# A third buffer for raw modulation weights, and low-part weight pieces loaded one piece earlier and stored one step later, in a two-layer attention and convolution backbone

## The chip, the cores and the metric

One core of a Trainium2 chip runs the whole program. The core has a matrix engine (PE, TensorE), a vector engine (DVE, VectorE), an activation engine (ACT, ScalarE), a general engine (POOL, GpSimd) and a queue engine (SP, SyncE) that here issues nearly all transfers (DMA) between device memory and the on-chip memory. Each engine works through its own instruction list in order and waits on semaphores for the others. The metric is the device time of one execution in microseconds (us); the kernel before takes 1704.04 us, the median of 3 runs (1703.88 to 1704.39).

## The reference, cut to what matters

Two layers: windowed attention with a context prefix, then a convolution module. All of it is fp32. Cut to the parts that the change touches or runs beside:

```python
D_MODEL, SEQ, CTX_LEN = 1024, 1024, 256
N_Q_HEADS, N_KV_HEADS, HEAD_DIM, WINDOW = 16, 4, 128, 128
# layer i: modulation of the tokens from the condition c
shift, scale, gate = split(silu(c) @ ada_w[i] + ada_b[i], 3)
h = rmsnorm(x, norm_g[i]) * (1 + scale) + shift
# layer 0: attention; q, k, v, z are columns of one projection
q, k, v, z = split(h @ attn_w_in)             # k, v also of the context
p = softmax over [sink, 256 context keys, latent keys within +-128]
x = x + gate * ((p @ [v_ctx, v]) * silu(z)) @ attn_w_out   # attn_w_out: 2048 x 1024
# layer 1: gated pointwise, depthwise convolution of width 31, layer norm, swish
x = x + gate * (u * silu(z)) @ conv_w_out                  # conv_w_out: 2048 x 1024
out = rmsnorm(x, final_g)
```

## The kernel before

**Arithmetic.** A matmul operand in fp32 is written as the sum of a high part (the rounding to `F32R`, made by an ACT copy) and a low part (the remainder, a subtraction on POOL or DVE). Each product is then three matmuls: high by high, high by low, low by high. So every weight piece needs an ACT copy and a subtraction before PE can use it.

**The attention stage** is a loop over 128 steps, 16 heads by 8 blocks of 128 queries (L1154). A step issues `scores` of the next block (6 matmuls into a PSUM tile `pss`, a masked maximum on DVE, an exponential on ACT, a scaling of `p_page` on POOL), then 12 matmuls of the next projections (`fill`), every fourth step the product with the values (`pv`), and then `transposes` of this step's block (4 or 5 PE transposes of `p_page` into `pss`, an ACT copy into `pthi`, a DVE subtraction into `ptlo`). PE keeps the program's order there; the other engines are ordered by the scheduler of the framework when the program is built, from its own estimate of times, and that order is then fixed. Where a key and value group ends (after heads 3, 7 and 11) the step is a regrouping: it projects `k` and `v` of the next group (`job`), with an ACT copy `vf_half` of each part of `v` that PE then transposes.

**Two background tasks** are generators that the loop advances by one `yield` a step:

- `ada_rest` (L604) adds up the rest of the modulation, silu(c) @ ada_w, in 128 pieces of 128x256 numbers (128 KB). Each piece is loaded by SP into one of two raw buffers, `dww_raw` and `wsum_raw` (places that the convolution uses later), and then multiplied and added on DVE. The load of piece i+1 is issued in the step that uses piece i; its buffer is the one that piece i-1 was read from.
- `low_parts` (L663) makes the low parts of the two output projections, `attn_w_out` and `conv_w_out`, in 32 pieces of 128x2x512 (512 KB): load into a page `low`, twice an ACT copy into a half page `lhi` and a POOL subtraction back into the page, then a store to device memory (`wolA`, `wolC`), from where later stages read it. A piece takes three turns: in the first the load is issued, and after it the store of the piece before (`store`, L657); in the second and third the two halves are split. A step with no turn for `low_parts` calls `store` (L1170).

**Memory.** `Pages` hands out 45 pages of 4 KB a partition and 6 half pages in rotation: a page is taken from the front of the free list and goes to its end when it is freed. Who gets a page waits for the last reader of its former content. `lhi`, `rope`, `oz` and `vf` share the half pages; `low`, `p`, `wraw` (raw projection weights) and others share the pages.

**SP's queue** holds, in one list, the loads of raw projection weights (`wraw_page`), the modulation pieces, the low pieces, their stores, and the stores `ozd` of the attention's output. An entry that waits holds up all entries behind it.

Of the kernel before, what the change touches and what calls it, by code (L numbers as in the profile page):

```python
# [9 lines left out]
F32 = mybir.dt.float32  # L10
# [4 lines left out]
P = 128  # L15
# [79 lines left out]
def backbone_kernel(  # L95
# [14 lines left out]
    cpool = ctx_stack.enter_context(tc.tile_pool(name="cpool", bufs=1))  # L110
    pgpool = ctx_stack.enter_context(tc.tile_pool(name="pages", bufs=1))
    hfpool = ctx_stack.enter_context(tc.tile_pool(name="halves", bufs=1))
    ps = ctx_stack.enter_context(tc.tile_pool(name="ps", bufs=2, space=PSUM))
    dr = ctx_stack.enter_context(tc.tile_pool(name="dr", bufs=1, space=bass.MemoryType.DRAM))
    pg = Pages(pgpool, 45, "page", 1024)
# [456 lines left out]
    def vt_split(vf, n, dh, dl):  # L572

        tp = ps_o(*vbank)
        for i in range(n // P):
# [16 lines left out]
    acc_a = mask_pg[:, 768:1024]  # L592
    ada_raw = [cpool.tile([P, n], F32, tag=t, name=t + "_raw", bufs=1)[:, 0:256]
               for t, n in (("dww", NJ * TAPS), ("wsum", NJ * 16))]

    anchor = []
    anchor_p = []
# [6 lines left out]
    def ada_rest():  # L604
        todo = [(l, c0) for l, c0 in [(0, 2048 + 256 * i) for i in range(4)] + [(1, 256 * i) for i in range(12)]]
        todo = [(l, c0, kt) for l, c0 in todo for kt in range(KT)]

        def load(i):
            l, c0, kt = todo[i]
            SY.dma_start(out=ada_raw[i % 2], in_=ada_w[l, kt * P:(kt + 1) * P, c0:c0 + 256])  # L610

        load(0)
        bank = ps_o(1)
        acc, o = bank[:, 0:256], bank[:, 256:512]
        for i, (l, c0, kt) in enumerate(todo):
            if i + 1 < len(todo):
                load(i + 1)
            raw = ada_raw[i % 2]
            if kt == 0:
                after(V.tensor_scalar(out=acc, in0=raw, scalar1=cs[:, kt:kt + 1], scalar2=None, op0=ALU.mult))  # L620
                for b in range(2):
                    col = (c0 - 2048 if l == 0 else 1024 + c0) // P + b
                    bs = slice(b * P, b * P + P)
                    stt(acc[:, bs], ident, abt[:, col:col + 1], acc[:, bs], ALU.mult, ALU.add)
            else:
                after(stt(acc, raw, cs[:, kt:kt + 1], acc, ALU.mult, ALU.add))
            yield
            if kt < KT - 1:
                continue
            V.tensor_copy(acc_a, acc)  # L630
            yield "copied"
            if i + 1 == len(todo):
                yield
            if c0 >= 2048:
                PE.matmul(o[0:1], ones[:, 0:1], acc_a, start=True, stop=True)
                V.tensor_copy(acc_a[0:1], o[0:1])
                SY.dma_start(out=gd[l][:, c0 - 2048:c0 - 1792], in_=acc_a[0:1])
            else:
                for b in range(2):
                    PE.matmul(o[:, b:b + 1], acc_a[:, b * P:b * P + P], ones[:, 0:1], start=True, stop=True)  # L640
                V.tensor_copy(mod1[:, c0 // P:c0 // P + 2], o[:, 0:2])

    adag = ada_rest()


# [17 lines left out]
    def low_parts():  # L663

        items = [(pair_rows(w, m, kk), d[m, kk]) for w, d in ((Wo, wolA), (Wp, wolC)) for m in range(2) for kk in range(NK)]
        for src, dst in items:
            raw = pg.alloc(F32, [2, 512], "low")
            SY.dma_start(out=raw, in_=src)
            store()
            yield "open"  # L670
            for b in range(2):
                hi = hp.alloc(F32R, None, "lhi")
                act(hi[:, 0:512], raw[:, b], AF.Copy)
                after(split_lo(G, raw[:, b], raw[:, b], hi[:, 0:512]), anchor_p)
                hp.free(hi)
                if b == 0:
                    yield "open"
            made.append((dst, raw))
            yield "shut"
        store()  # L680

    subs = [(h, m) for h in range(2) for m in range(2)]
    seqB = [(s, kk) for s in range(len(subs)) for kk in range(NK)]
# [1109 lines left out]
```

## Time and profile before

The median of the runs shown is 1704.04 us. The profiled execution took 1702.68 us in itself, of which the span from its first to its last instruction is 1700.9 us. One execution was profiled; all sums are made against it.

| what | number |
|---|---|
| runs, median (lowest to highest) | 1704.04 us (1703.88 to 1704.39) |
| profiled execution, its own time | 1702.68 us |
| its span | 1700.9 us |
| granted clock of PE, mean | 0.999 |
| attention stage | about 75 to 826 us of the span |
| first and last conversion of a low piece | 113.7 and 714.7 us |
| DMA, mean over the span | 143 GB/s |
| low pieces, median from issue to landing | 4.0 us (`attn_w_out`), 4.8 us (`conv_w_out`) |

How to read it: busy time is counted when an instruction of the engine runs. Rows for the DMA queues (SPq, ACTq) stand for the issue of a transfer, not for its duration. In a row of the timeline, the text in brackets is the idle time of that engine just before the instruction and what ended it. Matmuls overlap: a row of 0.39 us is followed by the next matmul 0.23 us later, so a wait of PE shorter than the overlap does not show as idle time.

### The profile page before, as it was taken

The page shows a single profiled execution, that of the slowest core. Times are in us where ns is not written, and L with a number is a line of the kernel's source. Part 1 is how long each engine was busy: PE and PEld are TensorE (multiplying, and loading weights), DVE is VectorE, ACT ScalarE, POOL GpSimd, SP SyncE. Part 2 cuts the span into 40 slices and gives each one's busy share as a digit, 9 for nine tenths or more (in the row PEclk, how much of TensorE's full clock was granted, in tenths as well). Part 3 has the DMA queues.
Part 4 walks back from the last instruction along what each step waited for, and adds up shares of the span by engine and source line. Part 5 has one row for each costly group of instructions (what it writes and reads, how often), then busy time and mean ns, then how long its engine had stood idle before and what let it go on. Part 6 is the DMA issues. An engine that isn't in the chain of part 4 may idle for free.

```text
span 1700.9 us, 23976 instructions
## 1 busy us (share of the span) xinstructions
PE 1684.5 (99%) x8490; PEld 1420.9 (84%) x8490; DVE 1091.3 (64%) x2074; ACT 877.9 (52%) x1538; POOL 882.5 (52%) x732
## 2 busy tenths in 40 slices
PE   9999999999999999999999999999999999999997
PEld 6888888888888888888888888888888888888886
DVE  5755544555355544556215289999999999868922
ACT  6755544555345544446234355665665664566831
POOL 0256653666456554643001167999898888130400
PEclk9999999999999999999999999999999999999999
DMA  9334442444334532437776622010111202377981
GB/s 383 93 100 140 140 124 92 143 155 140 97 119 147 160 121 91 140 118 266 279 252 216 243 81 99 14 62 25 62 63 43 88 32 81 124 266 250 331 271 50
DMA packets 109848, 242.46 MB, mean 143 GB/s; under 512 B 11306, under 2 KB 28002, under 8 KB 109728
## 3 DMA queue, kind: packets, MB, share of 16 engines
q1 hardware_dynamic: 103328, 230.43, 39.7%
q10 hardware_dynamic: 6400, 10.49, 2.5%
q8 instruction: 67, 1.10, 0.3%
q14 instruction: 53, 0.43, 0.1%
HBM read 188.70 MB, written 41.69 MB: 135 GB/s over the span
## 4 chain that ended last, share of the span: by engine, by line
PE 92%; DMA 4%; ACT 1%; issue 1%; DVE 1%; POOL 1%; SPq 0%; ACTq 0%; POOLq 0%; DVEq 0%
PE psg L89 48%; PE pss L89 24%; PE pso L89 20%; DMA araw_page<-in_k_ada_dram 2%; DMA low_page<-in_conv_w_out_dram 1%; DMA rope_half<-rope_half 1%; DMA dww_raw<-in_ada_w_dram 0%; ACT lhi_half L89 0%; POOL rope_half L89 0%; SPq L89 0%; DMA low_page<-in_attn_w_out_dram 0%; DVE ptlo L89 0%; ACT pthi L89 0%; ACT p_page L89 0%; ACT rope_half L89 0%
## 5 line engine op out<-in xcount | busy, mean ns | idle before, releaser
L89 POOL TENSOR_TENSOR odd_half<-odd_half,prod_half 128x513 f32<-128x513 f32 (+2 forms) x252 | 314.2, 1254 | 23.0 <-ACT prod_half L89 9.6
L89 PE MATMUL psg<-hh_page,whi_page 128*128 128x512 f32 x600 | 235.6, 393 | 0.0
L89 PE MATMUL psg<-hl_page,whi_page 128*128 128x512 f32 x600 | 234.5, 391 | 0.0
L89 PE MATMUL psg<-hh_page,wlo_page 128*128 128x512 f32 x600 | 234.0, 390 | 0.0
L89 ACT ACTIVATE prod_half<-ubuf,dww 128x513 f32<-128x513 f32 (+2 forms) x252 | 165.5, 675 | 116.0 <-POOL odd_half L89 112.2
L89 POOL TENSOR_TENSOR wlo_page<-wraw_page,whi_page 128x512 fp32r<-128x512 f32 (+1 forms) x104 | 172.9, 1679 | 92.0 <-ACT whi_page L89 79.6
L89 POOL TENSOR_SCALAR p_page<-p_page,sc 128x640 f32<-128x640 f32 (+1 forms) x128 | 99.3, 776 | 221.2 <-DVE sc L89 215.2
L89 PE MATMUL psg<-h2h_page,whi_page 128*128 128x512 f32 x464 | 181.9, 392 | 0.0
L89 PE MATMUL psg<-h2h_page,wlo_page 128*128 128x512 f32 x464 | 180.6, 389 | 0.0
L89 PE MATMUL psg<-h2l_page,whi_page 128*128 128x512 f32 x464 | 180.6, 389 | 0.0
L89 DVE SCALAR_TENSOR_TENSOR pss<-ubuf,dww,pss 128x512 f32<-128x512 f32 (+3 forms) x270 | 172.8, 673 | 0.1
L89 DVE SCALAR_TENSOR_TENSOR pss<-ubuf,wsum,pss 128x512 f32<-128x512 f32 (+3 forms) x270 | 172.2, 673 | 0.2
L89 DVE TENSOR_TENSOR ptlo<-pss,pthi 128x640 fp32r<-128x640 f32 (+1 forms) x144 | 103.5, 719 | 85.9 <-ACT pthi L89 84.6
L89 ACT ACTIVATE pthi<-pss 128x640 fp32r<-128x640 f32 (+1 forms) x144 | 88.8, 617 | 105.3 <-PE pss L89 98.8
L89 ACT ACTIVATE p_page<-p_page,sc 128x641 f32<-128x641 f32 (+1 forms) x128 | 102.6, 802 | 75.4 <-DVE sc L89 71.7
L89 PEld LDWEIGHTS psg<-hh_page,wlo_page 128*128 128x128 f32 x600 | 112.7, 188 | 24.5
L89 PEld LDWEIGHTS psg<-hh_page,whi_page 128*128 128x128 f32 x600 | 112.7, 188 | 19.4
L89 PEld LDWEIGHTS psg<-hl_page,whi_page 128*128 128x128 f32 x600 | 112.8, 188 | 18.5
L89 ACT ACTIVATE whi_page<-wraw_page 128x1024 fp32r<-128x1024 f32 x88 | 92.6, 1052 | 53.6 <-PE psg L89 19.9
L89 PE MATMUL pso<-h2h_page,whi_page 128*128 128x512 f32 x304 | 118.3, 389 | 0.0
L89 PE MATMUL pso<-h2l_page,whi_page 128*128 128x512 f32 x304 | 118.3, 389 | 0.0
L89 PE MATMUL pso<-h2h_page,wlo_page 128*128 128x512 f32 x304 | 118.3, 389 | 0.0
(254 smaller groups left out, 3999.6 us busy)
## 6 DMA issues: line engine op xcount, KB each, us to landing
wraw_page<-in_k_wconv_dram SPq DMA_DIRECT2D x48, 512.0 KB, 3.3
wraw_page<-in_k_win_dram SPq DMA_DIRECT2D x40, 512.0 KB, 3.8
wol_page<-wolA SPq DMA_DIRECT2D x32, 512.0 KB, 6.3
wo_page<-in_attn_w_out_dram SPq DMA_DIRECT2D x32, 512.0 KB, 5.8
wo_page<-in_conv_w_out_dram SPq DMA_DIRECT2D x32, 512.0 KB, 4.8
wol_page<-wolC SPq DMA_DIRECT2D x32, 512.0 KB, 6.2
rope_half<-rope_half ACTq DMA_DIRECT2D x80, 128.0 KB, 2.4
araw_page<-in_k_ada_dram SPq DMA_DIRECT2D x16, 512.0 KB, 10.3
```

What stands on the lines that cost most here:

```text
L89: r = f(*a, **k)
```

## The change

The raw modulation buffers become three: a tile of 128x256 in a pool of its own, `third_raw`, joins the two, and the pieces go round the three. The load of piece i+1 now goes into the buffer that piece i-2 was read from.

`low_parts` loads one piece ahead. Piece 0 is loaded in a first turn of its own. From then on the load of piece i+1 is issued between the two halves of piece i, and the store of piece i-1 right behind that load. A third turn of each piece does nothing, so a piece still takes three. With this the load stands three turns ahead of the first conversion, not one, and the store two turns behind the last conversion, not one.

```diff
+    expool = ctx_stack.enter_context(tc.tile_pool(name="extra", bufs=1))
...
     ada_raw = [cpool.tile([P, n], F32, tag=t, name=t + "_raw", bufs=1)[:, 0:256]
                for t, n in (("dww", NJ * TAPS), ("wsum", NJ * 16))]
+    ada_raw.append(expool.tile([P, 256], F32, tag="third", name="third_raw", bufs=1))
...
         def load(i):
             l, c0, kt = todo[i]
-            SY.dma_start(out=ada_raw[i % 2], in_=ada_w[l, kt * P:(kt + 1) * P, c0:c0 + 256])
+            SY.dma_start(out=ada_raw[i % 3], in_=ada_w[l, kt * P:(kt + 1) * P, c0:c0 + 256])
...
-            raw = ada_raw[i % 2]
+            raw = ada_raw[i % 3]
...
     def low_parts():
         items = [(pair_rows(w, m, kk), d[m, kk]) for w, d in ((Wo, wolA), (Wp, wolC)) for m in range(2) for kk in range(NK)]
-        for src, dst in items:
-            raw = pg.alloc(F32, [2, 512], "low")
-            SY.dma_start(out=raw, in_=src)
-            store()
-            yield "open"
+        raws = {}
+
+        def load(i):
+            if i < len(items):
+                raws[i] = pg.alloc(F32, [2, 512], "low")
+                SY.dma_start(out=raws[i], in_=items[i][0])
+
+        load(0)
+        yield "open"
+        for i, (_, dst) in enumerate(items):
+            raw = raws.pop(i)
             for b in range(2):
                 hi = hp.alloc(F32R, None, "lhi")
                 act(hi[:, 0:512], raw[:, b], AF.Copy)
                 after(split_lo(G, raw[:, b], raw[:, b], hi[:, 0:512]), anchor_p)
                 hp.free(hi)
                 if b == 0:
+                    load(i + 1)
+                    store()
                     yield "open"
             made.append((dst, raw))
             yield "shut"
+            yield "open"
         store()
```

PE's list of instructions is the same in both programs. On the other engines the same instructions stand in another order, from the start of the attention stage to its end. Three places follow (at the third, two engines); the names are the program's, with a running number.

SP's queue in head 10, before; the low piece that is converted next is `low_page_5619`:

```order
L89 DMA wraw_page_5590<-in_k_win_dram 128x1024
L89 DMA wsum_raw<-in_ada_w_dram 128x256
L89 DMA dww_raw<-in_ada_w_dram 128x256
L89 DMA wolC<-low_page_5452 128x1024
L89 DMA ozd<-oz_half_5554 128x512
L89 DMA low_page_5619<-in_conv_w_out_dram 128x2x512
L89 DMA low_page_5770<-in_conv_w_out_dram 128x2x512
```

And in the changed program, where the same piece is called `low_page_5509`:

```order
L89 DMA wolC<-low_page_5208 128x1024
L89 DMA dww_raw<-in_ada_w_dram 128x256
L89 DMA low_page_5509<-in_conv_w_out_dram 128x2x512
L89 DMA wsum_raw<-in_ada_w_dram 128x256
L89 DMA third_raw<-in_ada_w_dram 128x256
L89 DMA dww_raw<-in_ada_w_dram 128x256
L89 DMA ozd<-oz_half_5560 128x512
L89 DMA wraw_page_5596<-in_k_win_dram 128x1024
L89 DMA wolC<-low_page_5359 128x1024
```

The load of this piece stood behind the store of the piece before it and behind the `ozd` store; it now stands ahead of both, with three modulation loads between.

ACT's list at the same place, before (`pthi` serves the transposes of a step, the row with `sc` is an exponential):

```order
L89 ACTIVATE pthi<-pss_5557 128x2x128 x2
L89 ACTIVATE p_page_5578,sc_5579<-p_page_5578,sc_5579 128x641
L89 ACTIVATE lhi_half_5657<-low_page_5619 128x512
L89 ACTIVATE lhi_half_5706<-low_page_5619 128x512
L89 ACTIVATE pthi<-pss_5607 128x5x128
```

And in the changed program:

```order
L89 ACTIVATE lhi_half_5660<-low_page_5509 128x512
L89 ACTIVATE pthi<-pss_5497 128x4x128
L89 ACTIVATE whi_page_5591<-wraw_page_5176 128x1024
L89 ACTIVATE p_page_5519,sc_5520<-p_page_5519,sc_5520 128x641
L89 ACTIVATE zs_page_5483<-psg_5484 128x512
L89 ACTIVATE qh_page_5266<-rope_half_5460 128x512
L89 ACTIVATE lhi_half_5712<-low_page_5509 128x512
L89 ACTIVATE pthi<-pss_5563 128x2x128
L89 ACTIVATE p_page_5673<-nsink 128x1
L89 ACTIVATE pthi<-pss_5563 128x2x128
L89 ACTIVATE p_page_5584,sc_5585<-p_page_5584,sc_5585 128x641
L89 ACTIVATE pthi<-pss_5613 128x5x128
```

The two conversions stood side by side ahead of the `pthi` of one step; they now stand apart, one step and two steps earlier, and nothing stands between the exponential and that `pthi`.

ACT's list at the second regrouping (after head 7), before:

```order
L89 ACTIVATE pthi<-pss_4528 128x4x128
L89 ACTIVATE vf_half_4569<-psg_4537 128x256
L89 ACTIVATE kh_page_4419<-rope_half_4489 128x512
L89 ACTIVATE kvc_page_4421<-pso_4578 128x256
L89 ACTIVATE p_page_4669<-nsink 128x1
L89 ACTIVATE vf_half_4601<-psg_4571 128x512
```

And in the changed program:

```order
L89 ACTIVATE pthi<-pss_4534 128x4x128
L89 ACTIVATE kh_page_4425<-rope_half_4495 128x512
L89 ACTIVATE lhi_half_4731<-low_page_4248 128x512
L89 ACTIVATE vf_half_4575<-psg_4543 128x256
L89 ACTIVATE kvc_page_4427<-pso_4584 128x256
L89 ACTIVATE lhi_half_4872<-low_page_4734 128x512
L89 ACTIVATE lhi_half_4787<-low_page_4248 128x512
L89 ACTIVATE vf_half_4607<-psg_4577 128x512
```

Three conversions of low pieces moved ahead of the second `vf_half`, and the first `vf_half`, for which PE's next transposes wait, moved behind `kh` and one conversion.

POOL's list at the same place, before and in the changed program (`sin_page` marks the rope product that `kh` is made from, `kl_page` the low part of `k`):

```order
L89 TENSOR_TENSOR rope_half_4455<-rope_half_4455,sin_page_547 128x512
L89 TENSOR_TENSOR kl_page_4420<-rope_half_4456,kh_page_4419 128x512
L89 TENSOR_TENSOR rope_half_4488<-rope_half_4488,sin_page_547 128x512
L89 TENSOR_TENSOR wlo_page_4563<-wraw_page_4333,whi_page_4562 128x512 x2
L89 TENSOR_TENSOR kl_page_4420<-rope_half_4489,kh_page_4419 128x512
```

```order
L89 TENSOR_TENSOR rope_half_4461<-rope_half_4461,sin_page_550 128x512
L89 TENSOR_TENSOR ql_page_4222<-rope_half_4416,qh_page_4221 128x512
L89 TENSOR_TENSOR rope_half_4494<-rope_half_4494,sin_page_550 128x512
L89 TENSOR_TENSOR kl_page_4426<-rope_half_4462,kh_page_4425 128x512
L89 TENSOR_TENSOR wlo_page_4569<-wraw_page_4339,whi_page_4568 128x512 x2
L89 TENSOR_TENSOR kl_page_4426<-rope_half_4495,kh_page_4425 128x512
```

The second rope product moved ahead of the first `kl`.

Counted over ACT's two lists, a conversion stands directly ahead of a `pthi` 21 times before and 23 times in the changed program, and directly ahead of another conversion 10 times and 3 times. On POOL, the split of a projection weight that stood ahead of the last `p_page` of head 2 stands behind it, two steps later.

## The prediction

> **What bounds the kernel now.** I read the page's busy times first, then PE's busy time by stage, then PE's waits within the attention stage, which is the only stage that the change touches.
>
> ```profile
> span 1700.9 us, 23976 instructions
> PE 1684.5 (99%) x8490; PEld 1420.9 (84%) x8490; DVE 1091.3 (64%) x2074; ACT 877.9 (52%) x1538; POOL 882.5 (52%) x732
> ```
>
> ```profile
> 0.00:60.00 60.00, 55.40 (x359) 39.63 (x360) 35.06 (x86) 38.27 (x58) 3.70 (x9) 1.00 0.76 293
> 190.00:826.00 636.00, 633.17 (x3522) 551.08 (x3521) 322.45 (x708) 309.93 (x647) 345.97 (x322) 1.00 0.44 140
> 1450.00:1701.00 251.00, 241.93 (x1080) 199.78 (x1078) 157.43 (x299) 129.96 (x208) 41.76 (x28) 0.99 0.63 218
> ```
>
> PE is busy for 1684.5 of 1700.9 us. Of the 16.4 us of idle time, 4.6 lie in the first 60 us and 9.1 at the end (second number of a row is the stretch, third PE's busy time). The attention stage holds 636.00 - 633.17 = 2.8 us. That is all the idle time which this change can reach, and its PE list is the same as before, so the question is which of PE's waits go and which come.
>
> ```profile
> PE pss L89 <- DVE ptlo L89: 1.4, 1, 1.4
> PE pss L89 <- POOL p_page L89: 0.5, 1, 0.5
> PE pso L89 <- DVE ptlo L89: 0.5, 2, 0.2
> PE pso L89 <- ACT lhi_half L89: 0.3, 2, 0.2
> PE pso L89 <- DVE oz_half L89: 0.2, 1, 0.2
> ```
>
> These are PE's waits between 190 and 800 us: seven, 2.9 us, half of it in one. A wait costs more than its idle time, because matmuls overlap:
>
> ```profile
> 558.44 0.39 PE L89 MATMUL psg<-hh_page,wlo_page 128*128 128x512 f32 x1
> 558.67 0.71 PE L89 MATMUL pss<-ident,p_page 128*128 128x128 f32 x5
> 560.79 0.45 PE L89 MATMUL pss<-kh_page,qh_page 128*128 128x384 f32 x1 [1.41 <-DVE ptlo L89]
> ```
>
> A matmul of 0.39 us is followed 0.23 us later, so up to 0.2 us of each wait is hidden under the modelled end of the one before. Seven waits are then at most 2.9 + 7 x 0.2 = 4.3 us, 0.25% of the time. A difference of under 0.2%, 3.4 us, is about what a measurement of this kernel cannot tell from none; so a gain can hardly be a clear one.
>
> **Where the long wait comes from.** The timeline around it, and the chain of waits for the transfer:
>
> ```profile
> 549.87 1.31 POOL L89 TENSOR_TENSOR low_page<-low_page,lhi_half 128x512 f32<-128x512 f32 x1
> 551.21 0.33 SPq L89 DMA_DIRECT2D wolC<-low_page  x1
> 551.59 0.42 SPq L89 DMA_DIRECT2D ozd<-oz_half  x1
> 552.06 2.16 SPq L89 DMA_DIRECT2D low_page<-in_conv_w_out_dram  x2
> 558.13 1.15 ACT L89 ACTIVATE lhi_half<-low_page 128x512 fp32r<-128x512 f32 x2 [4.15 <-DMA low_page<-in_conv_w_out_dram]
> 559.19 0.68 ACT L89 ACTIVATE pthi<-pss 128x640 fp32r<-128x640 f32 x1
> ```
>
> ```profile
> 552.06 6.05 DMA low_page<-in_conv_w_out_dram
> ```
>
> POOL ends a low piece at 551.18; only then can SP issue its store, and behind the store stand `ozd` and the next piece's load, at 552.06. That load takes 6.05 us. ACT reaches its conversions and stands for 4.15 us; `pthi`, ready since the transposes of 558.67, comes behind both, then `ptlo`, then PE. So the load is late because it was issued late, and it was issued late because SP works in order. Over the whole stage:
>
> ```profile
>   DMA low_page<-in_attn_w_out_dram: 19.2, 11
>   DMA low_page<-in_conv_w_out_dram: 10.7, 7
> ```
>
> ```profile
> SPq L89 <- DVE pso L89: 154.5, 79, 9.5
> SPq L89 <- POOL low_page L89: 83.6, 30, 5.8
> ```
>
> The conversions wait for their loads 18 times, 29.9 us (most of it in ACT's slack, since PE loses only 2.9); SP waits 30 times for a low piece to be finished before its store and 79 times for DVE to have read a modulation buffer.
>
> **The change part by part.** *Third buffer.* No instruction is added; 128 loads go round three places. A load then needs the reader two pieces back, which is done a step earlier, so the 154.5 us of SP's waits shrink. Nobody waits behind them on PE's path by itself: worth nothing alone, but it lets the low loads behind them out earlier. If that cover were missing, the most would be the low loads' own waits below. *Loads ahead.* 32 loads move past one store each, past `ozd` stores and modulation loads, two turns earlier; by the order printed above, the load of the piece at 552.06 now stands in the queue where three more modulation loads come ahead of the `ozd` of 551.59. *Stores later.* 32 stores move one turn back, so that POOL has mostly finished when SP comes to them; the 83.6 us shrink. Nobody reads the stored pieces within the next steps; the price is one more page held, so a page is taken again sooner. A load that must wait for its page holds up SP, but raw projection weights and low pieces are now both taken well ahead: I take nothing, at worst one late piece as at 560.79, 1.65 us.
>
> What PE gets back, wait by wait. The long one: its five transposes end their starts at 558.67 + 4 x 0.11 = 559.11, so 560.79 is about 1.65 us late. The others, each with the row of its cause:
>
> ```profile
> 199.72 2.57 POOL L89 TENSOR_TENSOR wlo_page<-wraw_page,whi_page 128x512 fp32r<-128x512 f32 x2 [2.32 <-ACT whi_page L89]
> 203.02 0.66 PE L89 MATMUL pss<-ident,p_page 128*128 128x128 f32 x4 [0.47 <-POOL p_page L89]
> ```
>
> ```profile
> 504.33 1.31 ACT L89 ACTIVATE lhi_half<-low_page 128x512 fp32r<-128x512 f32 x2 [2.73 <-POOL low_page L89]
> 506.29 0.41 PE L89 MATMUL pso<-pthi,kvc_page 128*128 128x512 f32 x1
> 506.91 0.50 PE L89 MATMUL pso<-ptlo,kvc_page 128*128 128x512 f32 x1 [0.22 <-DVE ptlo L89]
> ```
>
> ```profile
> 697.67 0.63 ACT L89 ACTIVATE lhi_half<-low_page 128x512 fp32r<-128x512 f32 x1 [2.84 <-DMA rope_half<-rope_half]
> 698.92 0.41 PE L89 MATMUL pso<-pthi,kvc_page 128*128 128x512 f32 x1
> 699.57 0.50 PE L89 MATMUL pso<-ptlo,kvc_page 128*128 128x512 f32 x1 [0.23 <-DVE ptlo L89]
> ```
>
> ```profile
> 271.67 1.15 ACT L89 ACTIVATE lhi_half<-low_page 128x512 fp32r<-128x512 f32 x2 [2.12 <-DMA low_page<-in_attn_w_out_dram]
> 272.30 0.63 PE L89 MATMUL pso<-ident,vf_half 128*128 128x128 f32 x4 [0.17 <-ACT lhi_half L89]
> 655.08 0.63 PE L89 MATMUL pso<-ident,vf_half 128*128 128x128 f32 x4 [0.17 <-ACT lhi_half L89]
> ```
>
> At 203.02 a weight split of 2.57 us stands on POOL ahead of the step's `p_page`; in the new order it stands behind it: 0.47 + 0.16 = 0.63 us. At 506.91 the distance is 0.62 us where 0.23 is usual: 0.39. At 272.30 and 655.08 conversions behind their loads hold up PE: 2 x 0.17 = 0.34. At 699.57, 0.65 - 0.23 = 0.42, but here the conversion waits for a half page that a rope transfer still reads, and the half pages go round as before: I take half, 0.2. The sum is 1.65 + 0.63 + 0.39 + 0.34 + 0.2 = 3.2 us.
>
> What it puts in. Two things move conversions in front of PE's needs. At the second regrouping the first `vf_half` now comes behind `kh` and a conversion:
>
> ```profile
> 443.32 1.29 POOL L89 TENSOR_TENSOR kl_page<-rope_half,kh_page 128x512 fp32r<-128x512 f32 x1 [1.47 <-ACT kh_page L89]
> 447.71 0.63 ACT L89 ACTIVATE kh_page<-rope_half 128x512 fp32r<-128x512 f32 x1 [0.71 <-DVE rope_half L89]
> 447.81 0.38 PE L89 MATMUL pso<-ident,vf_half 128*128 128x128 f32 x2
> ```
>
> With `kh` at 447.71, `vf_half` (0.39 long, behind 0.54 and 0.58 of ACT, its starts being that far apart) ends at 449.2, 1.4 us after PE wanted it. On the other side, POOL's list there now has the second rope product ahead of the 1.29 us `kl` of 443.32, not behind it, so `kh` may come about that much sooner and the price be 0.2. Without a row that decides, I take the lower half, 0.5 (range 0.2 to 1.4). Elsewhere the 64 conversions go to other places in ACT's list; ahead of a `pthi` directly stand 23 where 21 did, and pairs of them are 3 where 10 were. I take 0.4 us for new small waits, two like those at 506.91 and 272.30 (bounds 0 and the 2.9 us that all waits now make). The net is -3.2 + 0.9 = -2.3 us. The profiled execution would take 1702.68 - 2.3 = 1700.4; the runs shown lie 1.36 us above it, so **1704.04 - 2.3 = 1701.7 us**.
>
> A rule of the Trainium skill speaks against any gain: its page "DMA: Bandwidth & Descriptors", section "Anatomy of one DMA", gives a transfer about 2.0 us plus its bytes at 436 GB/s, which is an estimate of 3.2 us for 512 KB. By that rule the load of 552.06 lands at 555.3, before the transposes of 558.67, PE waits for nothing, and the change is worth nothing. The trace does not agree, with 6.05 us from issue to landing; that fit is for another issuing path.
>
> **The rivals.** *The whole of it goes* (0.25): every one of the seven waits at its full length, 4.3 us, with no new ones. For it: pairs are broken up, loads come two turns earlier, and the runs shown are 1.36 us slower than the profiled one, which may be more such waiting. Against it: the waits for `oz_half` and for a rope half page have other causes. Time 1704.04 - 4.3 = 1699.7.
>
> *It doesn't do what it says* (0.10): the scheduler fills ACT's idle time, so it moves a conversion forward as soon as it believes the load has landed, and ACT waits as long, only elsewhere. For it: at the piece shown, the first conversion moved a step forward too. Against it: at that place `pthi` no longer has a conversion ahead. Time 1704 within 1 us.
>
> *Regroupings stall* (0.18), the other side: at each of the three, conversions stand ahead of a `vf_half`, and the last of them takes a half page that POOL's final `kl` must first have read. If POOL ends that `kl` one weight split later, 2.57 us, `vf_half` is some 2.3 us late and PE with it. Three times 2.3 is 6.9: 1704.04 - 3.2 + 6.9 = 1707.7. It decides from 1.1 us a regrouping on. For it: the long POOL list there. Against it: POOL stood idle after `kl` at the regroupings, and it has time for the rest:
>
> ```profile
> POOL p_page L89 <- DVE sc L89: 177.4, 63, 15.6
> ```
>
> That POOL waits 177.4 us for the softmax also says that a low split or weight split moved by a place is mostly free. The Trainium skill's page "TensorE: Matmul & The Clock Gate", section "Why this matters for your kernels", warns that an idle stretch of PE over about 3 us halves its clock; by it a long new stall would cost about its length again. The longest wait here is 1.41 us at a clock of 1.00, so no row shows it.
>
> **How the numbers follow.** The forecast, a gain of 2.3 us, has 0.47, and its own range is 1700.4 to 1703.5: credit 3.2, returns between 0 and 2.7. The larger gain has 0.25, no effect 0.10, stalls 0.18. Clearly faster (under 1700.6) is the larger gain and the low edge of the forecast, 0.25 + 0.05 = 0.30; slower (over 1707.4) is the stalls, most of them, 0.17; the rest is 0.53. The range 1699.0 to 1707.0 takes in the forecast, the larger gain and the lighter stalls, and leaves out about 0.15.
>
> **What would show it.** Right: PE's idle time in 190 to 826 us falls from 2.8 to about 1; no wait of 1.4 us for `ptlo`; conversions that wait for low loads a few times in place of 18; SP's waits for POOL's `low_page` well under 83.6 us. Wrong: PE waiting for `vf_half` at the regroupings by more than 1 us each, or PE's idle time unchanged with new rows of `lhi_half` behind a load. A time outside 1699 to 1707 would mean that something other than PE's waits in this stage moved.

## The result, and the profile after

The changed kernel takes 1707.51 us, the median of 13 runs (1706.54 to 1711.72). The kernel before, on the same chip, takes 1703.62 us (13 runs, 1702.24 to 1705.58). The ratio is 1.0026, with a 95% interval from 1.0019 to 1.0033: slower by about 4 us, a small loss but clear of the interval. The prediction was 1701.7 us with a range from 1699 to 1707, so both the sign and the range missed.

The profiled execution of the changed kernel took 1707.56 us itself, close to the median; that of the kernel before took 1702.68 us, 0.9 us under its median, so the two profiles differ by more (4.9 us) than the medians do (3.9 us). Its span and busy times, from the first part of the page:

```profile
span 1705.8 us, 23973 instructions
PE 1686.1 (99%) x8490; PEld 1419.6 (83%) x8490; DVE 1091.9 (64%) x2074; ACT 877.1 (51%) x1538; POOL 883.3 (52%) x732
```

The span is 4.9 us longer at the same work on every engine. The windows by stage (the stretch, then PE, PEld, DVE, ACT, POOL, the clock of PE, the DMA share and GB/s):

```profile
0.00:60.00 60.00, 54.93 (x360) 39.01 (x361) 35.20 (x87) 38.04 (x58) 3.71 (x9) 1.00 0.77 296
190.00:826.00 636.00, 630.39 (x3497) 546.14 (x3495) 319.88 (x706) 308.43 (x647) 345.40 (x314) 1.00 0.44 138
1450.00:1706.00 256.00, 246.81 (x1101) 203.89 (x1099) 161.25 (x304) 131.36 (x210) 42.41 (x28) 0.99 0.62 215
```

PE's idle time in the attention stage grew from 2.83 to 636.00 - 630.39 = 5.61 us; in the first 60 us it is 5.1 where it was 4.6, and at the end 9.2 where it was 9.1. Idle time shows only a part, because a wait also eats the overlap of matmuls. If one takes, for every PE instruction, the distance from the start of the one before it, and subtracts what is usual for that pair of instructions (the 15th percentile of all such pairs in the same trace), the sum between 190 and 826 us is 13.8 us before and 18.7 us now: 4.9 us more, which is the whole growth of the span. By stretch the sum grew by 2.2 us (190 to 285), 3.0 us (285 to 480), -0.8 us (480 to 674) and 0.5 us (674 to 826).

PE's waits between 190 and 800 us (in total, times, longest, all in us):

```profile
PE psg L89 <- DVE rope_half L89: 1.3, 1, 1.3
PE pso L89 <- ACT pthi L89: 1.2, 2, 0.8
PE pso L89 <- DVE ptlo L89: 1.1, 5, 0.2
PE pso L89 <- ACT vf_half L89: 0.9, 1, 0.9
PE pso L89 <- DVE oz_half L89: 0.5, 3, 0.2
PE pss L89 <- DVE sc L89: 0.4, 1, 0.4
```

The wait of 1.4 us that `pss` had for `ptlo` is gone, and so are the waits for `p_page` and `lhi_half`. New are waits of the product with the values (`pso`) for `pthi`, more of them for `ptlo` (5 where there were 2), one for a `vf_half`, and one for a rope half page. What ended the idle time of ACT and POOL in front of the instructions of a low piece, by tile, over the whole span (us, times):

```profile
  DMA rope_half<-rope_half: 21.4, 7
  POOL low_page L89: 9.9, 12
  DMA ozd<-oz_half: 4.3, 2
  DMA low_page<-in_attn_w_out_dram: 4.1, 3
```

Before, the same view had this row for rope transfers, besides 29.9 us for the loads:

```profile
  DMA rope_half<-rope_half: 6.1, 5
```

So the conversions hardly wait for their loads any more: 4.1 us where there were 29.9. Instead they wait 21.4 us for a rope transfer to leave the half page that they are to write. SP's waits for low pieces fell too, from 83.6 us, and bought nothing. Its waits for modulation buffers rose from 154.5 us, in spite of the third buffer:

```profile
SPq L89 <- POOL low_page L89: 51.6, 27, 6.5
SPq L89 <- DVE pso L89: 179.4, 86, 9.7
```

The later place of the stores in the program moved nothing by itself: in both kernels SP issues a store 0.03 us (median of 32) behind the end of POOL's last subtraction on the piece. What grew is the time from the load of a piece to its store, in which it holds its page: from 24.7 to 33.9 us in the median.

One of the new waits in the timeline, at a step where the product with the values follows:

```profile
351.06 0.38 SPq L89 DMA_DIRECT2D low_page<-in_attn_w_out_dram  x1
...
351.11 1.40 ACTq L89 DMA_DIRECT2D rope_half<-rope_half  x2
...
354.30 0.60 PE L89 MATMUL pss<-ident,p_page 128*128 128x128 f32 x4
...
358.13 0.39 PE L89 MATMUL psg<-hh_page,wlo_page 128*128 128x512 f32 x1
358.14 0.63 ACT L89 ACTIVATE lhi_half<-low_page 128x512 fp32r<-128x512 f32 x1 [4.67 <-DMA rope_half<-rope_half]
...
358.68 0.58 ACT L89 ACTIVATE pthi<-pss 128x512 fp32r<-128x512 f32 x1
...
359.31 0.49 PE L89 MATMUL pso<-pthi,kvc_page 128*128 128x512 f32 x1 [0.79 <-ACT pthi L89]
...
360.04 0.50 PE L89 MATMUL pso<-ptlo,kvc_page 128*128 128x512 f32 x1 [0.23 <-DVE ptlo L89]
```

(The row of 351.06, the load of a low piece just ahead of the two rope transfers, is taken up at e9.) PE has made the transposes by 354.9. ACT stands idle for 4.67 us ahead of the conversion, because its list has the conversion first; `pthi` comes 0.54 us behind it. PE starts the product 1.18 us after its last projection matmul where 0.23 us is usual, and then waits again for `ptlo`, 0.73 us where 0.23 is usual: 1.45 us in all. The same group stands at 207, 400, 552, 593 and 704 us. Whether such a wait costs anything depends on what stands behind the conversion. In the kernel before a conversion waits 2.65 us at the step of the group at 207 us, but `pthi` stands ahead of it there, not behind, and PE's product loses nothing:

```profile
207.05 0.63 ACT L89 ACTIVATE lhi_half<-low_page 128x512 fp32r<-128x512 f32 x1 [2.65 <-DMA low_page<-in_attn_w_out_dram]
...
207.35 0.39 PE L89 MATMUL pso<-ptlo,kvc_page 128*128 128x512 f32 x1
```

### The profile page after: what moved, and what is told of

Read it like the earlier page. It is cut to its first block, busy times and chain, and to the rows that moved or that the text cites. A ratio compares the mean times of both kernels' runs of the same rounds, so it can differ in the third digit from the quotient of the medians.

```text
span 1705.8 us, 23973 instructions
## 1 busy us (share of the span) xinstructions
PE 1686.1 (99%) x8490; PEld 1419.6 (83%) x8490; DVE 1091.9 (64%) x2074; ACT 877.1 (51%) x1538; POOL 883.3 (52%) x732
## 3 DMA queue, kind: packets, MB, share of 16 engines
q10 hardware_dynamic: 6400, 10.49, 2.5%
## 4 chain that ended last, share of the span: by engine, by line
PE 90%; DMA 4%; POOL 2%; ACT 2%; DVE 1%; issue 1%; SPq 0%; ACTq 0%; POOLq 0%; DVEq 0%
PE psg L89 45%; PE pss L89 24%; PE pso L89 21%; DMA rope_half<-rope_half 2%; DMA araw_page<-in_k_ada_dram 1%; POOL rope_half L89 1%; POOL wlo_page L89 1%; DMA wsum_raw<-in_ada_w_dram 0%; ACT pthi L89 0%; ACT rope_half L89 0%; DVE ptlo L89 0%; ACT lhi_half L89 0%; POOL ql_page L89 0%; POOL low_page L89 0%; DVE rope_half L89 0%
## 5 line engine op out<-in xcount | busy, mean ns | idle before, releaser
L89 POOL TENSOR_TENSOR rope_half<-rope_half,sin_page 128x512 f32<-128x512 f32 x40 | 52.6, 1315 | 130.0 <-DMA rope_half<-rope_half 118.3
```

The lines of the kernel that those rows point to most:

```text
L89: r = f(*a, **k)
```

## The experiments

Four theories were put to the chip. A: the loss comes from conversions that stand on ACT ahead of a `pthi` or `vf_half` and wait for a half page that a rope transfer still reads. B: the third modulation buffer carries it. C: the page that is held longer carries it. D, formed later: the early load itself makes the rope transfers late. All ratios are to the kernel before on the same chip. Its median was 1703.62 us beside the change, 1703.77 beside e1 to e4, 1704.42 beside e5 to e8 and 1703.61 beside e9 to e11, so medians of different groups should not be subtracted from each other.

| kernel | median us | ratio | 95% interval |
|---|---|---|---|
| the change | 1707.51 | 1.0026 | 1.0019 to 1.0033 |
| e1, third buffer alone | 1704.03 | 1.0002 | 0.9993 to 1.0011 |
| e2, `low_parts` alone | 1708.30 | 1.0022 | 1.0012 to 1.0032 |
| e3, change, store a turn sooner | 1705.85 | 1.0012 | 1.0003 to 1.0020 |
| e4, change, conversions into a page | 1707.27 | 1.0020 | 1.0011 to 1.0029 |
| e5, change, conversions behind `pthi` | 1701.81 | 0.9988 | 0.9979 to 0.9997 |
| e6, e5 with e3 | 1702.86 | 0.9996 | 0.9987 to 1.0004 |
| e7, before, store later alone | 1703.64 | 0.9995 | 0.9987 to 1.0004 |
| e8, before, conversions behind `pthi` | 1701.18 | 0.9982 | 0.9973 to 0.9991 |
| e9, change, load in two transfers | 1706.75 | 1.0018 | 1.0009 to 1.0026 |
| e10, change, load a turn later | 1705.94 | 1.0011 | 1.0002 to 1.0020 |
| e11, e8 with the third buffer | 1700.89 | 0.9984 | 0.9975 to 0.9993 |

**e1: the third buffer alone.** Against the kernel before:

```diff
+    ada_raw.append(expool.tile([P, 256], F32, tag="third", name="third_raw", bufs=1))
-            SY.dma_start(out=ada_raw[i % 2], in_=ada_w[l, kt * P:(kt + 1) * P, c0:c0 + 256])
+            SY.dma_start(out=ada_raw[i % 3], in_=ada_w[l, kt * P:(kt + 1) * P, c0:c0 + 256])
-            raw = ada_raw[i % 2]
+            raw = ada_raw[i % 3]
```

> The kernel before with the third modulation buffer alone; low pieces are loaded and stored as before. Theory A (the loss comes from conversions that stand ahead of pthi on ACT and wait for a half page that a rope transfer still reads): these come from the earlier loads, so no loss here: 1703.6 within 1.5 us, and the long wait for a late low load (1.65 us at 560.79 before) may stay. Theory B (the third buffer carries the loss, through another order on DVE and SP): about 1707.5.

No difference was measured: 1.0002, an interval that holds 1. SP's waits for modulation buffers did not shrink either, 156.0 us where there were 154.5. The conversions wait for their loads 37.1 us there, in 19 waits, no less than before:

```profile
  DMA low_page<-in_attn_w_out_dram: 19.7, 10
  DMA low_page<-in_conv_w_out_dram: 17.4, 9
```

**e2: the change of `low_parts` alone.** The changed kernel with `ada_raw[i % 2]` and without the third tile.

> The changed kernel with two modulation buffers, so the change of low_parts alone. Theory A: 1707.5 within 1.5 us, and conversions wait for rope transfers about 20 us in all, as in the changed kernel (21.4 us). Theory B: the loss is gone, about 1702 to 1703.6.

The whole loss is there, 1.0022, and with it the waits for rope transfers:

```profile
  DMA rope_half<-rope_half: 21.4, 8
```

B falls with e1 and e2.

**e3: the store a turn sooner.** Against the changed kernel:

```diff
             yield "shut"
+            store()
             yield "open"
```

> The changed kernel, but the third turn of a piece issues its store, so that its page is given back a turn or two earlier; loads stay one piece ahead. Theory A: 1707.5 within 1.5 us, conversions wait for rope transfers about 20 us. Theory C (the page that is held longer makes other pages come from places that are still read): at least 2 us are won back, 1705.5 or less, and waits of ACT's p_page and of SP for pages fall.

1705.85 us misses both forecasts, 1706 to 1709 and 1705.5 or less. It is 2.1 us slower than the kernel before and some 2 us better than the change, and the intervals of the two ratios just touch. By its trace the groups at 207, 400 and 704 us are gone, those at 358, 551 and 592 us stand. It is no test of C, however: the stores did not come sooner. SP issues them, as before, 0.03 us behind POOL's last subtraction, and a piece holds its page for 34.6 us in the median (33.9 in the changed kernel).

**e4: conversions into a page.** Against the changed kernel:

```diff
-                hi = hp.alloc(F32R, None, "lhi")
+                hi = pg.alloc(F32R, [1024], "lhi")
...
-                hp.free(hi)
+                pg.free(hi)
```

> The changed kernel, but the conversions write into a page of the 45 instead of a half page, so no rope transfer can hold them up; the six half pages go round among rope, oz and vf alone. Theory A: the 21.4 us of conversions waiting for rope transfers go to 0, PE's waits for pthi and ptlo behind them (3 to 4 us) go too, time 1702 to 1705. Theory C: one more page is in use at a time, so it is slower than the changed kernel, 1708 or more. Theory B: 1707.5.

The time missed what theories A and C gave: 1707.27 us. It is what B gave, which e1 and e2 exclude. The waits did what A gave. No conversion waits for a rope transfer, and no `pthi`, `vf_half` or rope row is left among PE's waits between 190 and 800 us:

```profile
PE pss L89 <- DVE ptlo L89: 3.6, 3, 1.8
PE pss L89 <- DVE sc L89: 0.7, 2, 0.4
PE pso L89 <- DVE oz_half L89: 0.5, 3, 0.2
```

In their place stand long waits of another cause, the longest of them here:

```profile
369.27 0.20 ACT L89 ACTIVATE p_page<-nsink 128x1 f32<-128x1 f32 x1 [1.72 <-DMA wolA<-low_page]
369.38 0.69 ACT L89 ACTIVATE pthi<-pss 128x640 fp32r<-128x640 f32 x1
...
371.07 0.74 PE L89 MATMUL pss<-ident,p_page 128*128 128x128 f32 x5 [1.76 <-DVE ptlo L89]
```

Here the first use of a new `p_page` waits until the store of a low piece has read that page, and `pthi` stands behind it. The pages have become scarce, because the conversions now take them as well. It is the same form of stall with another buffer: something that is early in ACT's list waits for a place in memory, and the `pthi` behind it pays. The clock has a part in e4 too. Behind the two longest of these waits of PE, 1.76 us at 371.07 and 1.45 us at 564.82, the granted clock is 0.50 for 3.41 us (columns as in the windows by stage; the clock is the third number from the end):

```profile
371.95:375.36 3.41, 3.20 (x10) 2.90 (x11) 2.37 (x8) 3.13 (x7) 2.01 (x2) 0.50 0.26 77
```

Projection matmuls start 0.43 us apart there where 0.23 is usual, and by the distances of PE's starts the stretches cost 1.5 and 1.6 us on top of the waits. Neither the kernel before nor the changed one has such a stretch between 190 and 800 us. The clock is not all of it: three executions of e4 have the mean clock of the kernel before's profile, 0.999, and still take 1706.6 to 1707.3 us. So e4 supports A in the waits, not in the time, and shows that C's mechanism exists, where pages are scarcer than in the changed kernel.

**e5: conversions behind `pthi`.** A dependency for the scheduler alone, against the changed kernel; `anchor_t` holds the last `pthi` issued when the conversion is written down, that is the one of the step before:

```diff
+    anchor_t = []
...
-                act(hi[:, 0:512], raw[:, b], AF.Copy)
+                after(act(hi[:, 0:512], raw[:, b], AF.Copy), anchor_t)
...
-            act(pthi[:, bs], tv[:, r0:r1], AF.Copy)
+            anchor_t[:] = [act(pthi[:, bs], tv[:, r0:r1], AF.Copy)]
```

> The changed kernel with one rule for the scheduler more: a conversion of a low piece stands on ACT behind the pthi of the step before its turn. PE's list, loads, stores and pages stay as in the changed kernel. Theory A (the loss comes from conversions that stand ahead of a pthi or vf_half on ACT and wait for a half page): the waits for pthi, and for ptlo behind it, at 207, 359, 400, 552 and 704 us go, about 4 us, so 1703 to 1704.5. Theory C (pages held longer): unchanged, 1707.5 within 1.5. If ACT were just overfull there, a conversion behind pthi would hold up the next exponential instead, and the time would be about the same or longer.

The time is 1701.81 us, below the time expected and 0.12% under the kernel before. Loads, stores, pages and half pages go round as in the changed kernel; the conversions start later, by 13.7 us in the median (4.2 to 30.1). None is left directly ahead of a `pthi` (23 in the changed kernel), and none waits: ACT has no idle time in front of any. So e5 removes the order and the waits together and does not say what either would do alone. The step shown above looks like this now:

```profile
353.45 0.60 ACT L89 ACTIVATE pthi<-pss 128x512 fp32r<-128x512 f32 x1 [1.47 <-PE pss L89]
...
353.95 0.62 ACT L89 ACTIVATE lhi_half<-low_page 128x512 fp32r<-128x512 f32 x1
...
356.87 0.39 PE L89 MATMUL pso<-pthi,kvc_page 128*128 128x512 f32 x1
356.89 1.29 POOL L89 TENSOR_TENSOR rope_half<-rope_half,sin_page 128x512 f32<-128x512 f32 x1 [3.77 <-DMA rope_half<-rope_half]
```

The rope transfer is as late as before: POOL, which needs it, waits 3.77 us and starts 7.2 us behind the issue of the two transfers (7.1 in the changed kernel). It costs PE nothing there, since `pthi` was done 2.8 us before PE wanted it. e5 also decides on C: a piece holds its page for 36.8 us in the median, longer than in the changed kernel (33.9), and nothing is lost. PE's remaining waits in the stage are 2.2 us (5.4 in the changed kernel):

```profile
PE psg L89 <- DVE rope_half L89: 0.9, 1, 0.9
PE pss L89 <- POOL p_page L89: 0.8, 1, 0.8
PE pso L89 <- DVE oz_half L89: 0.5, 3, 0.2
```

**e6: e5 with the sooner store of e3.**

> As e5, and the store of a piece is issued in its third turn (as in e3). Theory A alone: as e5, 1703 to 1704.5. Theories A and C together: the 1.7 us that e3 won come on top, 1701 to 1703, faster than the kernel before.

1702.86 us, not better than e5, so the gain of e3 does not add to the pin. Theory A alone gave 1703 to 1704.5, A and C together 1701 to 1703; the time falls into the second range, but e5 without that edit is faster still, so it does not speak for C. Here too a piece holds its page as long as in e5, 37.2 us.

**e7: the later store alone.** Against the kernel before:

```diff
             raw = pg.alloc(F32, [2, 512], "low")
             SY.dma_start(out=raw, in_=src)
-            store()
             yield "open"
...
                 if b == 0:
+                    store()
                     yield "open"
```

> The kernel before, but the store of a piece is issued two turns behind its last conversion (between the halves of the next piece); the load comes with its own piece as before, and there are two modulation buffers. Theory A: conversions still find their load as the last thing to arrive, so few wait for rope transfers (under 8 us), no loss, 1703.7 within 1.5 us. Theory C: the longer hold alone costs 1.5 us or more, 1705.2 or above. The load now goes to SP ahead of the store of the piece before, so the waits for loads should fall somewhat.

1703.64 us, no loss (the kernel before took 1704.42 beside it). As a test of C it is weak: the page is held for 27.2 us in the median, 2.5 us longer than before, where the change adds 9.2. Nor are PE's waits the same ones: those for `ptlo` are gone, and one of 1.7 us for `p_page` behind a weight split has come at 205 us. It is e5 with its longer hold by which C falls as the cause. The conversions wait for loads here, and hardly for rope transfers:

```profile
  DMA low_page<-in_attn_w_out_dram: 16.6, 9
  DMA low_page<-in_conv_w_out_dram: 9.2, 5
  DMA rope_half<-rope_half: 1.7, 3
```

Why e3, which differs from the change by the place of the store in the program alone, is 1.7 us faster is left open. It has fewer waits of conversions for rope transfers (16.7 us), so it may be a matter of which conversions fall ahead of which `pthi`; that was not shown.

**e8: the kernel before with the rule of e5.**

> The kernel before with the rule of e5. Here conversions wait for their loads: those that stand right ahead of a pthi no longer hold it up, so up to the 2.5 us of waits for pthi and ptlo at 507, 561 and 700 us go: 1701.2 to 1703.7. If it gains as much as e5 gains on the changed kernel, the place of conversions on ACT decides, whatever they wait for, and the change only traded one thing that they wait for against another.

1701.18 us, 0.9982 (0.9973 to 0.9991): the lower edge of what was expected, and faster than both kernels. Neither early loads nor late stores are in it. The rule gains 3.2 us on the kernel before and, by the two ratios, 0.9988/1.0026 = 0.9962, about 6.5 us on the changed one; with it both are alike within their intervals. The gains are not equal, and equal gains were the condition on record for saying that the change only traded one wait for another. They are near what the groups behind waiting conversions cost, by the distances of PE's starts: 2.5 us in the kernel before (at 506.91, 560.79 and 699.57) and 5.7 us in the changed one (4.7 us at the products and 1.0 at the second regrouping).

**e9: a low piece in two transfers.** Against the changed kernel; the first half is loaded with the first conversion, the second with the second:

```diff
-        def load(i):
+        def load(i, b):
...
-                SY.dma_start(out=raws[i], in_=items[i][0])
+                SY.dma_start(out=raws[i][:, b], in_=items[i][0][:, b])
...
+                load(i + 1, b)
                 if b == 0:
-                    load(i + 1)
                     store()
```

> The changed kernel, but a low piece is loaded in two transfers of 256 KB, one in each of the two turns that convert the piece before, in place of one of 512 KB. Theory D (the early load is what makes the half pages late: a rope transfer issued just behind a 512 KB load lands 5 to 6 us after its issue, where 2.4 us is the median): the rope transfers collide with half the bytes, conversions wait for rope transfers 10 us or less (21.4 in the changed kernel), time 1703.5 to 1706. If the rope transfers are late for another reason, about 20 us stay and the time is 1707.5 within 1.5 us.

1.0018, and the conversions wait as long as in the changed kernel:

```profile
  DMA rope_half<-rope_half: 20.6, 7
```

D's number, 10 us or less, missed, but the run does not test D. In the trace SP issues the two halves of a piece together, within 1.2 us for 31 of the 32 pieces, so the same 512 KB stand beside the rope transfer as before:

```profile
199.25 1.21 SPq L89 DMA_DIRECT2D low_page<-in_attn_w_out_dram  x2
```

What the traces on hand show speaks for D. At each of the six long waits of the changed kernel SP issued the load of a low piece between 0.9 us before and 0.2 us after the first of the two rope transfers (351.06 and 351.11 in the rows further up). Of the 80 rope transfers, 14 are issued within 1.5 us behind such a load in the changed kernel, 3 in the kernel before. In eleven traces landings of rope transfers are recorded: the 50 transfers that were issued within 1.5 us behind a 512 KB load, of a low piece or of projection weights, took 3.2 to 6.8 us (median 5.0), the other 166 took 2.2 to 4.7 (median 2.3). This was counted afterwards, and no run kept the loads away from the rope transfers on purpose, so D is likely but not shown.

**e10: the load a turn later.** Against the changed kernel:

```diff
-                if b == 0:
+                if b == 1:
                     load(i + 1)
+                else:
                     store()
```

> The changed kernel, but the load of the next piece is issued one turn later, with the conversion of the second half. Theory D: loads and rope transfers meet again, since a load comes every three steps whichever of them it is; the meetings only fall elsewhere: 1705 to 1708.5, conversions wait for rope transfers over 10 us. If only the one turn chosen were unlucky: under 8 us of such waits and 1703.7 or less.

1.0011, with 14.2 us of waits for rope transfers and 16.6 us for loads. Time and waits are as D gave them. The load stands 7.5 us ahead of the first conversion in the median (13.2 in the changed kernel, 4.5 in the kernel before), so some conversions again wait for it. At the three waits of over 2.5 us for a rope transfer, the load of a low piece was again issued 0.3 to 0.9 us ahead of the transfers.

**e11: e8 with the third buffer.**

> The kernel before with the third modulation buffer and the rule of e5. The third buffer moved nothing measurable alone (e1), so with the rule it should move nothing either: the time of e8, ratio 0.998 to the kernel before within 0.001. If the waits of SP for the modulation buffers were worth anything, 0.997 or less.

0.9984: the time of e8 within the interval. The third buffer is worth nothing measurable, with the rule as without it.

## Why the prediction was wrong, point by point

**What bounds the kernel** held: the distances of PE's starts grew by 4.9 us in the attention stage, and no other part of the program changed by more than 0.5 us.

**The long wait.** The prediction gave 1.65 us for the wait of `ptlo` at 560.79. It is gone, and so is the 0.39 us at 506.91. The reason given for them was right too: conversions wait 4.1 us for low loads, not 29.9. SP waits 51.6 us for POOL's `low_page`, not 83.6, but not because POOL "has mostly finished when SP comes": 28 of the 32 stores still go within 0.1 us of POOL's end (31 before). And SP's waits for modulation buffers, which were to shrink, rose to 179.4 us.

**The other credits** were mostly not paid. The 0.63 us for `p_page` at 203.02 went, but waits of 0.55 and 0.15 us came at 215 and 224 us, ahead of other transposes (the first has DVE's `sc`, from the masked maximum, as its releaser). The 2 x 0.17 us at the regroupings stayed with another releaser: the row of `oz_half` (the attention's output) has 3 waits where it had 1. The wait of 0.42 us at 699.57, half of which was to go, is 0.66 us at 704.

**The second regrouping** was foreseen, with 0.5 us in a range from 0.2 to 1.4. It is 1.03 us, and by the mechanism named: `kh` and a conversion ahead of the first `vf_half`.

```profile
451.54 0.63 ACT L89 ACTIVATE kh_page<-rope_half 128x512 fp32r<-128x512 f32 x1 [1.04 <-DVE rope_half L89]
452.08 0.61 ACT L89 ACTIVATE lhi_half<-low_page 128x512 fp32r<-128x512 f32 x1
452.60 0.37 ACT L89 ACTIVATE vf_half<-psg 128x256 f32<-128x256 f32 x1
...
453.02 0.44 PE L89 MATMUL pso<-ident,vf_half 128*128 128x128 f32 x2 [0.88 <-ACT vf_half L89]
```

**The step that failed** is the next sentence of the prediction, "I take 0.4 us for new small waits", with bounds of 0 and 2.9. By the distances of PE's starts, the groups behind a waiting conversion cost 0.70 us at 207, 1.45 at 359, 0.50 at 400, 1.09 at 552, 0.27 at 593 and 0.66 at 704: 4.7 us. The rows of one of the smaller ones:

```profile
400.21 0.51 PE L89 MATMUL pso<-pthi,kvc_page 128*128 128x512 f32 x1
400.94 0.50 PE L89 MATMUL pso<-ptlo,kvc_page 128*128 128x512 f32 x1 [0.22 <-DVE ptlo L89]
```

The distance is 0.73 us where 0.23 is usual. The prediction had the mechanism on its page, at 699.57: a conversion that "waits for a half page that a rope transfer still reads, and the half pages go round as before". It counted one case of 0.42 us, half of which would go. But what a conversion waits for is the latest of its input and its output's place. Before, that was most often the load (18 waits of 42); with the load made early, the half page is the latest (and likely later than it was, as said at e9), so five waits for rope transfers, of 6.1 us in all, became seven of 21.4 us. The prediction removed a wait and did not ask what is late next for the instruction that had waited. e5 shows that the loss goes when the conversions stand behind `pthi`; e1, e2 and e7 that the waits for rope transfers come with the early loads (5.5, 21.4 and 1.7 us); e4 that without the half page they vanish, though other waits kept the time from coming back. That the scheduler set conversions so because its estimate of the rope transfer is shorter than what the chip shows fits the timeline, but was only argued.

**The balance.** By the distances of PE's starts, 3.1 us went (1.65 at 560.79, 0.63 at 203.02, 0.42 at 699.57, 0.40 at 506.91) and 7.7 us came (the 4.7 above, 1.3 more at the first regrouping, 1.0 at the second, 0.7 at 215 and 224); the net of 4.6 us is nearly the whole growth of 4.9.

**The range.** The prediction's own sum had a slip: with returns of 0.2 to 1.4 us at the regrouping and 0 to 2.9 us elsewhere, a credit of 3.2 us gives 1701.0 to 1705.1 us, not 1700.4 to 1703.5. The measured time lies above that too, since the small waits alone, at 4.7 us, are above their bound of 2.9. Its starting point, 1704.04 us from three runs, is 0.4 us above the median of thirteen. And it took 0.2% for what a measurement cannot tell from none, where the interval of the ratio is 0.07% to either side.

**Of the remainder**, 1.3 us is one wait at the first regrouping, where DVE's rope product waits for a half page that POOL's `ql` reads:

```profile
253.44 1.27 POOL L89 TENSOR_TENSOR ql_page<-rope_half,qh_page 128x512 fp32r<-128x512 f32 x1
...
255.49 0.39 PE L89 MATMUL psg<-hch_page,whi_page 128*128 128x256 f32 x1 [1.33 <-DVE rope_half L89]
```

In the kernel before it costs 0.24 us there, in e1 it costs 1.3 as well, where no loss in total was measured, in e5 still 1.2, and in e10 it does not occur. Its cause was not followed, so this part of the loss stays open.

**The rivals.** "The whole of it goes" is out: PE's idle time in the stage doubled. "Regroupings stall" gave 1707.7 us, which is the time that came, but by luck and not for its reason: the conversions wait for POOL's `kl` only 1.5 us in all, and the second `vf_half` of a regrouping does not hold up PE. "It doesn't do what it says" was wrong, since the load waits did go; yet its sentence that ACT would wait "as long, only elsewhere" was the nearest to what happened (ACT's idle time ahead of conversions fell from 54.7 to 43.4 us, in other places). The prediction's last sign of being wrong did not hold either: the time lies outside 1699 to 1707 us, and yet it was PE's waits in this stage that moved.

For a stalled PE's clock the prediction had no row. e4 has one: 0.50 for 3.41 us behind waits of 1.76 and 1.45 us, shorter ones than the prediction had in mind, at a price of 1.5 and 1.6 us, about their length again. The Trainium skill's page "DMA: Bandwidth & Descriptors", section "Issuing engines are not separate DMA queues", says that transfers issued by different engines run on the same 16 DMA engines and interleave. The changed kernel's trace agrees with it: the rope transfers go on queue q10 of the page (10.49 MB, 80 times 128 KB), the loads on q1, and beside the six rope transfers that took 4.5 us or more q1 moved 0.33 to 0.56 MB in their first 2.2 us, beside the 13 that took 2.4 us or less at most 0.12 MB.

## What to carry to other kernels

When a wait is removed by bringing one input earlier, look for the next latest input of the same instruction (here its output buffer), count how often it will decide, and see what stands behind the instruction on its engine. On an engine that works in order, the place of a background instruction that may wait can count for more than how long it waits: here ACT's idle time ahead of conversions fell by 11 us, and what it cost PE rose. One rule that set the conversions behind the softmax work, and so later, beat both kernels, with the late loads and with the early ones. Before an experiment is read, look in its trace whether the edit took place: the stores of e3 and the halves of e9 were moved in the program and hardly on the chip. And a rotation of buffers shared by a background task and the main loop links waits that the source code does not show.

## What the runs showed of the hardware

The spread of the rope transfers was not expected. They are all of 128 KB and issued by the same engine, and the median from issue to landing is 2.3 us in the changed kernel; the slowest take 6.1 us there and 5.1 us in the kernel before. Six conversions of the changed kernel waited over 2.5 us for a half page; for four of them (at 205.6, 399.0, 591.7 and 701.5 us) the landing of the transfer is recorded, and it came 5.0 to 6.1 us after the issue. What goes with it is a 512 KB load issued just ahead: within 1.5 us behind one, 50 transfers of eleven traces took 3.2 to 6.8 us, the other 166 took 2.2 to 4.7. That the load is the cause was not tested.

The granted clock of PE fell to 0.50 for 3.41 us in e4 behind waits of 1.76 and 1.45 us, and stayed at 1.00 between 190 and 800 us in the kernel before, whose longest wait is 1.41 us there.
